# The first tile's output stored as two and six rows a partition instead of four and four

## The chip, the cores and the metric

The kernel runs on one core of one Trainium2 chip. The metric is the device time in microseconds (us) of one execution, as the median of several. A profile's span is about 1.3 us shorter than the time of the run (467.9 against 469.19 us in the profiled run of the kernel before), so spans are compared with spans and times with times.

## The reference

```python
# x: float32 (32, 512, 2048), i.e. 16384 rows of 2048
x1, x2 = x[..., :1024], x[..., 1024:]
gelu_x1 = 0.5 * x1 * (1 + erf(x1 / np.sqrt(2)))
return (gelu_x1 * x2).astype(np.float32)      # (32, 512, 1024)
```

134.22 MB are read and 67.11 MB written.

## The kernel before

Sixteen tiles, each of 128 partitions with 8 rows. Loads are issued by SP (`nc.sync`), stores by ACT (`nc.scalar`) up to tile 13, and by SP after that. ACT computes GELU, DVE (`nc.vector`) multiplies in place. There are two input and two output buffers, and the loads and stores of one buffer share the semaphore `ready[k]`.

```python
for ins in (
    load(0, slice(0, 4), first[0]),      # L0a: rows 0-3 of every partition
    load(0, slice(4, 8), first[1]),      # L0b
    load(1, slice(0, 8), ready[1]),      # L1
):
    ...
for i in range(n_tiles):
    k = i % 2
    last = i == n_tiles - 1
    pieces = i == 0 or last
    steps = ((0, 2), (2, 4), (4, 8)) if pieces else ((0, 5), (5, 8))
    for lo, hi in steps:
        ...                              # ACT: wait for the input, GELU of these rows
        ...                              # DVE: multiply these rows
        if pieces and hi % 4 == 0:
            if last:
                store(nc.sync, i, slice(hi - 4, hi), tail_stored)
            else:
                store(nc.scalar, i, slice(hi - 4, hi), ready[k])
    if not pieces:
        ...                              # store all 8 rows, tile 14 on nc.sync
    if i + 2 < n_tiles:
        nc.sync.wait_ge(mul_done, n[mul_done.name])
        load(i + 2, slice(0, R), ready[k])
```

`store` makes its queue wait for all multiplies issued so far. So the first store of tile 0 follows the multiply of rows 2-3, the second that of rows 4-7.

Of the kernel before, what the change touches and what calls it, by code (L numbers as in the profile page):

```python
# [1 line left out]

# [4 lines left out]

GELU = mybir.ActivationFunctionType.Gelu


@with_exitstack
def kernel(
    ctx: ExitStack,
    tc: tile.TileContext,
    x: bass.AP,
    out: bass.AP,
):
    nc = tc.nc
    P = nc.NUM_PARTITIONS

    x_flat = x.flatten_outer_dims()
    out_flat = out.flatten_outer_dims()
    n_rows, dim = x_flat.shape
    half = dim // 2

    R = 8
    x_t = x_flat.rearrange("(n p r) d -> n p r d", p=P, r=R)
    o_t = out_flat.rearrange("(n p r) d -> n p r d", p=P, r=R)
    n_tiles = x_t.shape[0]
    x_bufs = [nc.alloc_sbuf_tensor(f"x{k}_tile", [P, R, dim], x.dtype) for k in range(2)]  # L30
    o_bufs = [nc.alloc_sbuf_tensor(f"o{k}_tile", [P, R, half], out.dtype) for k in range(2)]



    first = [nc.alloc_semaphore(f"first{j}") for j in range(2)]
    ready = [nc.alloc_semaphore(f"ready{k}") for k in range(2)]
    gelu_done = nc.alloc_semaphore("gelu_done")
    mul_done = nc.alloc_semaphore("mul_done")
    tail_stored = nc.alloc_semaphore("tail_stored")
    n = {sem.name: 0 for sem in [*first, *ready, gelu_done, mul_done, tail_stored]}  # L40

    def counted(ins, sem, by):
        ins.then_inc(sem, by)
        n[sem.name] += by

    def load(i, rows, sem):
        ins = nc.sync.dma_start(out=x_bufs[i % 2][:, rows, :], in_=x_t[i][:, rows, :])  # L47
        counted(ins, sem, 16)
        return ins

    def store(queue, i, rows, sem):
        queue.wait_ge(mul_done, n[mul_done.name])
        counted(
            queue.dma_start(out=o_t[i][:, rows, :], in_=o_bufs[i % 2][:, rows, :]), sem, 16
        )




    for ins in (  # L60
        load(0, slice(0, 4), first[0]),
        load(0, slice(4, 8), first[1]),
        load(1, slice(0, 8), ready[1]),
    ):
        tc.no_tile_sem_insts.add(ins.ins.name)
    tc.close()
    tc.compile()  # L67
# [7 lines that stand above are left out]
            rows = slice(lo, hi)  # L75
            if i == 0 and lo % 4 == 0:
                nc.scalar.wait_ge(first[lo // 4], 16)
            elif lo == 0:
                nc.scalar.wait_ge(ready[k], n[ready[k].name])
            counted(  # L80
                nc.scalar.activation(  # L81
                    out=o_bufs[k][:, rows, :], in_=x_bufs[k][:, rows, :half], func=GELU
                ),
                gelu_done,
                1,
            )
            nc.vector.wait_ge(gelu_done, n[gelu_done.name])
            counted(
                nc.vector.tensor_mul(  # L89
                    out=o_bufs[k][:, rows, :],  # L90
                    in0=o_bufs[k][:, rows, :],
                    in1=x_bufs[k][:, rows, half:],
                ),
                mul_done,
                1,
            )
            if pieces and hi % 4 == 0:
                if last:
                    store(nc.sync, i, slice(hi - 4, hi), tail_stored)
                else:  # L100
                    store(nc.scalar, i, slice(hi - 4, hi), ready[k])
        if not pieces:
            if i == n_tiles - 2:
                store(nc.sync, i, slice(0, R), tail_stored)
            else:
                store(nc.scalar, i, slice(0, R), ready[k])
# [5 lines that stand above are left out]
    nc.scalar.drain()  # L112
    for sem in (*first, *ready):
        nc.scalar.sem_clear(sem)
    nc.vector.drain()
    nc.vector.sem_clear(gelu_done)
    nc.sync.sem_clear(mul_done)
    nc.sync.wait_ge(tail_stored, n[tail_stored.name]).then_inc(
        tail_stored, -n[tail_stored.name]
    )  # L120


# [1 line left out]
_INS = ['x']  # L124
_OUTS = [((32, 512, 1024), 'float32')]


# [23 lines left out]
```

## Time and profile before

| | before |
|---|---|
| time, median of 3 runs | 469.26 us (469.24 to 469.31) |
| span of the profiled execution | 467.9 us |
| busy DVE, ACT | 30%, 25% of the span |
| packets of the two data queues | 99.7% of 16 DMA engines' span |
| period of a middle tile | 29.0 us |

Read the queues first: their packets fill 99.7% of the DMA engines' span, and no compute engine is busy for more than 30% of it. The prediction below shows the lines for that. These two lines of the timeline of the kernel before (start, length, engine, line, what) are the last stores and the last tile's GELUs:

```profile
432.86 27.74 SPq L54 DMA_DIRECT2D out_dram<-o_tile  x3
448.56 7.21 ACT L81 ACTIVATE o_tile<-x_tile 128x2048 f32<-128x2048 f32 x3 [21.87 <-DMA out_dram<-o_tile]
```

The last tile's computing begins at 448.56, while tile 14's store, issued at 432.86, is still being moved.

### The profile page before, as it was taken

How to read it: one execution, taken by the hardware profiler on the slowest of the kernel's cores; microseconds unless marked ns; L12 is line 12 of the kernel's file. 1: busy time of each engine (PE TensorE's matmuls, PEld its weight loads, DVE VectorE, ACT ScalarE, POOL GpSimd, SP SyncE). 2: the span in 40 equal slices, each digit the busy share in tenths (PEclk: the TensorE clock that was granted, in tenths of full speed). 3: DMA queues.
4: the chain of work that ended last, by engine and by line, in shares of the span. 5: the costliest groups of instructions: out<-in, count | busy, mean ns of one | idle time of the engine just before them, and what ended most of it. 6: DMA issues, size and time to landing. Idle time of an engine off the chain costs nothing.

```text
span 467.9 us, 152 instructions
## 1 busy us (share of the span) xinstructions
DVE 140.5 (30%) x34; ACT 115.5 (25%) x35; POOL 0.2 (0%) x4
## 2 busy tenths in 40 slices
DVE  0330514207052060511606116060150702507043
ACT  1320606042060410604106050050500506014060
POOL 0000000000000000000000000000000000000000
DMA  8999999999999999999999999999999999999998
GB/s 359 448 448 443 403 405 492 409 403 448 459 437 403 434 417 493 403 403 448 476 420 403 445 406 493 403 406 445 487 409 403 445 451 448 403 434 417 493 389 373
DMA packets 5041, 201.34 MB, mean 430 GB/s; under 512 B 560, under 2 KB 560, under 8 KB 560
## 3 DMA queue, kind: packets, MB, share of 16 engines
q1 hardware_dynamic: 2880, 142.61, 70.6%
q10 hardware_dynamic: 2160, 58.72, 29.1%
q14 instruction: 1, 0.01, 0.0%
HBM read 134.22 MB, written 67.11 MB: 430 GB/s over the span
## 4 chain that ended last, share of the span: by engine, by line
DMA 76%; DVE 14%; ACT 8%; ACTq 0%; SPq 0%; issue 0%
DMA out_dram<-o_tile 66%; DVE o_tile L89 14%; DMA x_tile<-in_x_dram 10%; ACT o_tile L81 8%; ACTq L112 0%; SPq L47 0%
## 5 line engine op out<-in xcount | busy, mean ns | idle before, releaser
L89 DVE TENSOR_TENSOR o_tile<-o_tile,x_tile 128x5120 f32<-128x5120 f32 (+3 forms) x34 | 140.5, 4171 | 319.7 <-ACT o_tile L81 319.7
L81 ACT ACTIVATE o_tile<-x_tile 128x5120 f32<-128x5120 f32 (+3 forms) x34 | 114.3, 3407 | 337.4 <-DMA out_dram<-o_tile 301.6
L81 ACT ACT_TABLE_LOAD x1 | 1.3, 1283 | 2.9 <-PEq L67 2.9
L135 POOL MEMSET const-bfloat16-1.0<- 128x1 bf16 x1 | 0.1, 101 | 0.0
L135 POOL MEMSET const-uint8-127<- 128x1 uint8 x1 | 0.1, 101 | 0.0
L135 POOL MEMSET const-float32-0.0<- 128x1 f32 x1 | 0.1, 98 | 0.2 <-issue 0.2
L135 POOL MEMSET const-float32-1.0<- 128x1 f32 x1 | 0.1, 98 | 0.0
## 6 DMA issues: line engine op xcount, KB each, us to landing
out_dram<-o_tile ACTq DMA_DIRECT2D x13, 4096.0 KB, 44.7
x_tile<-in_x_dram SPq DMA_DIRECT2D x2, 4096.0 KB, 16.6
out_dram<-o_tile ACTq DMA_DIRECT2D x2, 2048.0 KB, 34.5
out_dram<-o_tile SPq DMA_DIRECT2D x1, 4096.0 KB, 25.2
out_dram<-o_tile SPq DMA_DIRECT2D x2, 2048.0 KB, 7.8
x_tile<-in_x_dram SPq DMA_DIRECT2D x15, 44.2
```

The costliest lines, as they stand in the source:

```text
L81: nc.scalar.activation(out=o_bufs[k][:, rows, :], in_=x_bufs[k][:, rows, :half], func=GELU),
L89: nc.vector.tensor_mul(out=o_bufs[k][:, rows, :], in0=o_bufs[k][:, rows, :], in1=x_bufs[k][:, rows, half:],),
L135: nc = _bacc.Bacc("TRN2", target_bir_lowering=False, num_devices=1)
```

## The change

The intent: get the first bytes of output on their way earlier. The first store no longer waits for rows 2-3. It takes rows 0-1 as soon as they are multiplied, and the second store takes the other six rows. The loads stay.

```diff
-            if pieces and hi % 4 == 0:
-                if last:
-                    store(nc.sync, i, slice(hi - 4, hi), tail_stored)
-                else:
-                    store(nc.scalar, i, slice(hi - 4, hi), ready[k])
+            if last and hi % 4 == 0:
+                store(nc.sync, i, slice(hi - 4, hi), tail_stored)
+            elif i == 0 and hi != 4:
+                store(nc.scalar, i, slice(0, 2) if hi == 2 else slice(2, 8), ready[k])
```

## The prediction

> **What bounds the kernel now.** I read the page first: the span, the busy shares and the DMA lines. Its columns are plain; q1 is the queue that SP issues to (all loads and the last three stores), q10 the one that ACT issues to (all other stores).
>
> ```profile
> span 467.9 us, 152 instructions
> ...
> DVE 140.5 (30%) x34; ACT 115.5 (25%) x35; POOL 0.2 (0%) x4
> ...
> q1 hardware_dynamic: 2880, 142.61, 70.6%
> q10 hardware_dynamic: 2160, 58.72, 29.1%
> ...
> HBM read 134.22 MB, written 67.11 MB: 430 GB/s over the span
> ```
>
> No compute engine is busy over 30%, and the two queues' packets fill 70.6 + 29.1 = 99.7% of the 16 DMA engines' span. Next the busy time by window (window, its length, DVE, ACT, POOL busy, TensorE clock, DMA share, GB/s), to see whether that average hides a slow stretch:
>
> ```profile
> 1.74:467.40 465.66, 140.49 (x34) 115.54 (x35) 0.00 (x0) 1.00 1.00 432
> 22.00:47.00 25.00, 4.42 (x1) 3.62 (x1) 0.00 (x0) 1.00 1.02 435
> 47.00:71.00 24.00, 8.76 (x2) 7.12 (x2) 0.00 (x0) 1.00 1.00 434
> 100.56:216.56 116.00, 35.04 (x8) 28.49 (x9) 0.00 (x0) 1.00 1.00 434
> 216.56:332.56 116.00, 35.04 (x8) 28.49 (x9) 0.00 (x0) 1.00 1.00 434
> ```
>
> From its first packet, at 1.74 us in the packet records, to the last, ending at 467.42, the DMA moves 432 GB/s, and 434 in the long middle. All bytes at 434 GB/s are 201.33 MB / 434 = 463.9 us. The span has 4.0 us more: 1.74 before the first packet, 0.45 after the last, and about 1.8 spread over the first and last stretches. So about 1.8 us (0.4%) is all that an earlier or later store could touch at all.
>
> The chain of waits (start, length, what) seems to say something else, and has to be read with care:
>
> ```profile
> 60.50 40.04 DMA out_dram<-o_tile
> 100.53 0.02 issue
> 100.56 4.48 ACT o_tile L81
> 105.03 0.02 issue
> 105.06 8.77 DVE o_tile L89 x2
> 113.83 0.02 issue
> 113.85 44.68 DMA out_dram<-o_tile
> ```
>
> It shows store, GELU, multiply, store. But the 44.68 us of a store are mostly queueing: a 4.19 MB store at 434 GB/s is 9.7 us of work. The period is 29.0 us a tile (100.56 to 129.57 in the timeline), which is 12.58 MB / 434 GB/s = 29.0. The compute pieces of this chain run while loads move; the chain names who let ACT go, not what is scarce.
>
> The start, from the timeline (start, length, engine, line, what, idle time before it in brackets):
>
> ```profile
> 12.76 3.71 ACT L81 ACTIVATE o_tile<-x_tile 128x2048 f32<-128x2048 f32 x2 [8.62 <-DMA x_tile<-in_x_dram]
> 14.70 4.49 DVE L89 TENSOR_TENSOR o_tile<-o_tile,x_tile 128x2048 f32<-128x2048 f32 x2 [14.70 <-ACT o_tile L81]
> 19.23 0.38 ACTq L54 DMA_DIRECT2D out_dram<-o_tile  x1
> 22.46 3.62 ACT L81 ACTIVATE o_tile<-x_tile 128x4096 f32<-128x4096 f32 x1 [5.99 <-DMA x_tile<-in_x_dram]
> 30.57 0.36 ACTq L54 DMA_DIRECT2D out_dram<-o_tile  x1
> ```
>
> The half-tile load ends at 12.7, two pieces are computed, the first half is stored from 19.23; the second from 30.57.
>
> [...] from about 24 to 71 us each engine alternates one 65,536-byte load packet (2.42 us) with one 16,384-byte store packet (0.61 us), 346 and 87 GB/s, which is 4:1. [...]
>
> **The change part by part.** Write L0a, L0b for the halves of tile 0's load, Lk for later loads, Sk for stores. Each DMA is 128 packets, 8 per engine, one for each partition, so packet size follows the rows per partition.
>
> Bytes: unchanged. Packets: still two stores of 128 for tile 0; 16 KB + 16 KB become 8 KB + 24 KB. From 0.611 us for 16 KB and 1.213 us for 32 KB the fixed part of a packet is 2 x 0.611 - 1.213 = 0.009 us. As the count stays, tile 0's stores cost each engine 8 x (0.611 + 0.611) = 9.8 us before and, by estimate, 8 x (0.31 + 0.91) = 9.8 after.
>
> First store: it follows the first multiply, 14.70 + 2.29 = 16.98, so it is issued at about 17.0, 2.2 us earlier. The order on ACT changes with it: this store now sits between the GELUs of rows 0-1 and rows 2-3, and ACT waits there for DVE. Rows 2-3 start at 17.0 + 0.38 = 17.4, where they started at 14.58: 2.8 us later. They end near 19.3 and their multiply near 21.5. That costs nothing, as rows 4-7 wait for L0b until 22.46.
>
> L0b: before, the first store packets came at 24.4, 5.2 us after the issue, though each engine's L0b was already over at about 21.8 and one L1 packet had slipped in. [...] Issued at 17.0 it gets 0 to 2 packets of 0.31 us in ahead of L0b's end. L0b lands 0 to 0.6 us later, and so do the GELU of rows 4-7 (22.5 to 23.1), S0b and the issue of L2 (30.6 to 31.2).
>
> L2's issue: L2 stands on SP's queue behind L1, whose packets last until about 46.6. It has 16 us to spare; 0.6 us is hidden.
>
> Pairing: before, S0a went beside L1, S0b beside L2, S1 beside L3 and so on, in step. If k = 0 to 2 packets of S0a (perhaps 3) go beside L0b, every later store runs k packets ahead of its load: L1 would end 1 to 3 us earlier (beside smaller store packets), L2 and all middle loads up to k x 1.21 = 2.4 to 3.6 us later, as each has let k more 32 KB packets by. In the steady state a store waits about 15 us on its queue before its first packet; being k x 3.63 us early leaves at least 4.
>
> The end: S14 is issued on SP's queue[...]. Whatever the pairing, what moves before L15 ends is L0 to L15 and S0 to S13, the same bytes, so L15 ends where it did, near 448. Then S14 (9.7 us alone) and both halves of S15 run. The last tile's first half store is issued at 455.03, while S14's packets last until about 457.6: 2.6 us to spare. If tile 15 now waits for L15 and no longer for S13, it starts up to 0.4 us earlier, which is hidden too.
>
> Sum: bytes 0, packets 0, rows 2-3 hidden, L0b's delay hidden, end 0. The first store's 2.2 us give nothing: the DMA had load packets to move in that time. Expected: 0.0 us, with some tenths for how the engines happen to line up.
>
> **The rivals.** First, the intent holds: writing starts 2.2 us sooner and the end comes 2.2 us sooner, 467.1 us. For it: there is about 1.8 us of lower rate at start and end. Against it: that is less than 2.2, part of it is the first packets and the last engines' finish, and no window has the DMA waiting for a store. A part of a dip just after L0b (about 0.3 us) could go: 468.9.
>
> Second, ACT's wait in the middle becomes the bound: rows 2-3 run past L0b's landing and the second half is late. It has 22.46 - 19.3 = 3.2 us to spare on ACT and 16 at L2's issue. Exposed in full, 2.8 us would give 472.1; I see no path for it.
>
> Third, packets of 8 KB cost more than their share. If each took 0.1 us more than 0.31, 8 of them per engine would cost 0.8 us: 470.1. Nothing measured here points to it.
>
> Fourth, the shifted pairing makes a hole later or exposes the last tile's compute. The spare times above (4 us a tile, 2.6 us at the end) speak against it; a hole of 1 us would give 470.3.
>
> **Range and chances.** The runs before differ by 0.07 us. I predict 469.2 us, from 468.6 (the dip goes, with some luck at the end) to 469.8 (dearer packets or a worse finish of the engines). 2% is 9.4 us; no rival comes near it. Faster 0.01, within 2% 0.98, slower 0.01.
>
> **What would show it.** Right: first store issued near 17.0, rows 2-3 starting near 17.4, rows 4-7 at 22.5 to 23.1, 434 GB/s in the middle, a 29.0 us period, some ACT waits naming the load where they named the store, the last GELUs at 448.1 to 448.6, and a span of 467 to 469. Wrong: a window after 22 us well below 434 GB/s, or the last store's issue after S14's end.

## The result

| | before | after |
|---|---|---|
| time, median of 6 runs | 469.25 us (469.17 to 469.39) | 469.88 us (469.65 to 470.47) |
| span of the profiled execution | 467.9 us | 468.5 us |
| last data packet ends (packet records) | 467.42 us | 468.06 us |

The ratio is 1.0014, with a 95% interval of 1.0001 to 1.0027. A ratio here is the mean time of one kernel's fast runs over that of the other's of the same rounds, so not quite the ratio of the medians. By the medians the change makes the kernel 0.63 us slower; no run of one kernel lies in the range of the other's. The prediction had said 469.2 us, and 469.8 at the most. It was wrong, by a loss of less than 0.2% that it did not see.

The page of the changed kernel looks almost the same:

```profile
span 468.5 us, 152 instructions
...
DVE 140.6 (30%) x34; ACT 115.7 (25%) x35; POOL 0.2 (0%) x4
...
q1 hardware_dynamic: 2880, 142.61, 70.6%
q10 hardware_dynamic: 2160, 58.72, 29.0%
```

Same packets, same bytes, the DMA still full (70.6 + 29.0 = 99.6%, against 99.7% before). The busy share can't show the loss: a packet that takes longer than usual counts as busy.

The issues of DMA in the page of the changed kernel (what, queue, count, KB each, us from issue to landing) show the two pieces:

```profile
out_dram<-o_tile ACTq DMA_DIRECT2D x1, 3072.0 KB, 42.6
out_dram<-o_tile ACTq DMA_DIRECT2D x1, 1024.0 KB, 25.3
```

The start in the changed kernel's timeline:

```profile
12.85 1.91 ACT L81 ACTIVATE o_tile<-x_tile 128x2048 f32<-128x2048 f32 x1 [8.71 <-DMA x_tile<-in_x_dram]
14.79 2.29 DVE L89 TENSOR_TENSOR o_tile<-o_tile,x_tile 128x2048 f32<-128x2048 f32 x1 [14.79 <-ACT o_tile L81]
17.12 0.38 ACTq L54 DMA_DIRECT2D out_dram<-o_tile  x1
17.54 1.91 ACT L81 ACTIVATE o_tile<-x_tile 128x2048 f32<-128x2048 f32 x1 [2.78 <-DVE o_tile L89]
19.48 2.29 DVE L89 TENSOR_TENSOR o_tile<-o_tile,x_tile 128x2048 f32<-128x2048 f32 x1 [2.40 <-ACT o_tile L81]
23.76 3.62 ACT L81 ACTIVATE o_tile<-x_tile 128x4096 f32<-128x4096 f32 x1 [4.30 <-DMA x_tile<-in_x_dram]
```

The first store is issued at 17.12 instead of 19.23. ACT waits 2.78 us for DVE in front of rows 2-3, as foreseen. But rows 4-7 start at 23.76 instead of 22.46: L0b landed 1.3 us later, where 0 to 0.6 had been predicted.

The chain of waits of the changed kernel (start, length, what) answers to the one of before:

```profile
60.57 42.87 DMA out_dram<-o_tile
...
103.47 4.48 ACT o_tile L81
...
116.76 44.68 DMA out_dram<-o_tile
...
161.47 4.48 ACT o_tile L81
```

Tile 3's GELU starts at 103.47 instead of 100.56, 2.9 us later. That is the shift of the pairing (each load lets more store packets by), not a loss: the period after it is still 29.0 us (161.47 - 103.47 = 58.0 for two tiles). The chain still names the store as what released ACT. Loads and stores of a buffer share one semaphore here, and the packet records say otherwise: at tile 2 the last packet of S0b (the second store of tile 0) ended at 66.6 and that of L2 at 72.9, and ACT went on at 74.47. The name on a shared semaphore has to be checked against the packets.

The busy time by window (window, length, DVE, ACT, POOL busy, TensorE clock, DMA share, GB/s) over the long middle is equal. Before:

```profile
50.00:448.00 398.00, 122.65 (x28) 96.92 (x28) 0.00 (x0) 1.00 1.00 433
```

After:

```profile
50.00:448.00 398.00, 122.65 (x28) 97.01 (x28) 0.00 (x0) 1.00 1.00 433
```

So the time was lost in the first 50 us and carried to the end. The tail of the changed kernel in its timeline:

```profile
435.76 25.32 SPq L54 DMA_DIRECT2D out_dram<-o_tile  x3
449.04 7.22 ACT L81 ACTIVATE o_tile<-x_tile 128x2048 f32<-128x2048 f32 x3 [19.45 <-DMA out_dram<-o_tile]
```

The last GELUs start 0.48 us later than before (449.04 against 448.56).

**Where in the first 50 us.** The packet records have the queue, size, start and duration of each packet. Most packets of one size take the same time in every trace: 0.309 us for 8 KB, 0.611 for 16, 0.912 for 24, 1.213 for 32, 2.418 for 64. The records do not name the DMA engine, but joining each packet to the one that starts where it ends gives one engine's sequence. One engine before (L = load, S = store, KB, start and duration in us; the 4-byte packets that end each transfer, 16 for each, are left out):

```
L32 19.22 1.21 | L32 20.43 1.21 | L64 21.65 2.80 | S16 24.45 0.61 | L64 25.05 2.44 | S16 27.49 0.61 | L64 28.10 2.42 | ...
... S16 42.67 0.61 | L64 43.27 2.42 | S16 45.69 0.61 | L64 46.31 2.43 | S16 48.73 0.61 | L64 49.34 2.42
```

One engine after:

```
L32 17.98 1.21 | L32 19.19 1.88 | L32 21.07 1.26 | S8 22.33 0.31 | S8 22.64 0.31 | L64 22.95 2.42 | S8 25.36 0.31 | ...
... S8 38.96 0.31 | L64 39.27 2.42 | L64 41.69 2.83 | S24 44.51 0.91 | S24 45.42 0.91 | L64 46.33 2.42 | S24 48.75 0.91
```

In both, a load packet shortly ahead of the first store's first packet is stretched: 2.80 us for 2.42 before, 1.88 for 1.21 after. All 16 engines show it; before, it is the last load packet ahead of the store, after, the last or the one before the last. In the changed kernel there is a second such place, 2.83 for 2.42, where the second store begins. Store packets are not stretched: the longest of the changed kernel takes what most of its size take, and in the kernel before none is more than 0.02 us over that. (Two store packets that seem to follow each other, as S8 at 22.33 and 22.64, have the 4-byte packet that ends the load between them.)

I call "loss" the duration of the packets above the median of their size in the same trace, summed over all packets that start in a stretch and divided by 16 engines. In the first place (17 to 30 us) it is 0.33 us before and 0.62 after, in the second (30 to 50 us) 0.06 and 0.34. Together that is 0.39 and 0.96: 0.57 us more, of the 0.64 us by which the last packet ends later. From 50 us on it is under 0.05 us in both. The mean end of the last 16 packets is 0.58 us later, so the rest is how unevenly the engines finish. The loss leaves out time in which an engine has no packet at all; between 3 and 460 us there is next to none in these two traces, where the packets' times add up to 100.2% of that stretch on 16 engines (the records overlap a little).

### The profile page after: what moved, and what is told of

The parts are those of the page before. It is cut to its first block, busy times and chain, and to the rows that moved or that the text cites. A ratio compares the mean times of both kernels' runs of the same rounds, so it can differ in the third digit from the quotient of the medians.

```text
span 468.5 us, 152 instructions
## 1 busy us (share of the span) xinstructions
DVE 140.6 (30%) x34; ACT 115.7 (25%) x35; POOL 0.2 (0%) x4
## 3 DMA queue, kind: packets, MB, share of 16 engines
q1 hardware_dynamic: 2880, 142.61, 70.6%
q10 hardware_dynamic: 2160, 58.72, 29.0%
## 4 chain that ended last, share of the span: by engine, by line
DMA 76%; DVE 14%; ACT 8%; ACTq 0%; SPq 0%; issue 0%
DMA out_dram<-o_tile 66%; DVE o_tile L89 14%; DMA x_tile<-in_x_dram 10%; ACT o_tile L81 8%; ACTq L111 0%; SPq L47 0%
```

## The experiments

Where five rounds were asked for, 4 to 6 runs gave times; in the last three kernels three rounds gave 4. Times of kernels of one group are compared with the kernel before in the same rounds: its medians were 469.16, 469.19, 469.27 and 469.35 us in the four groups. The losses come from each kernel's one trace, so a difference of some 0.1 us between two of them means little.

**The theories.** A: the first loss grows because the store stream starts while tile 0's second half is still loading. B: the sizes of the store packets, small ones or a step from small to large, cost. C: the loss at the first store is the first use of ACT's DMA queue. D: it is ACT's wait in the middle. And chance, which needs repeats.

### The changed kernel again (after_again), the kernel before again (before_again)

No edit.

> The changed kernel, unaltered, to see whether its 0.6 us is the same each time. The trace so far puts the loss into two places: load packets stretched beside the start of the first store (18 to 24 us from the span's start, 0.64 us against 0.32 before) and load packets stretched around the change from the first store to the second (39 to 47 us, 0.35 us against about 0). If these are properties of the kernel, 469.7 to 470.0 us and both places again. If they are chance, one or both are missing from this trace and the time nears 469.3 us.

Measured: 469.97 us (469.69 to 470.26) against 469.16; losses 0.48 and 0.48 us. Both places are there again, so they belong to the kernel. How they divide is not fixed.

> The kernel before, unaltered, for a second trace of its own. If its one loss at the first store (0.3 us at 21 to 27 us) and the absence of one at the second are properties of the kernel, both are seen again; time 469.1 to 469.4 us.

Measured: 469.27 us, the same as the other runs of before in these rounds, with one run at 471.43. Losses 0.26 and 0.08 us. The one loss at the first store is seen again, and none at the second.

### Two and six rows, but issued as late as before (late26)

```diff
-            elif i == 0 and hi != 4:
-                store(nc.scalar, i, slice(0, 2) if hi == 2 else slice(2, 8), ready[k])
+            elif i == 0 and hi != 2:
+                store(nc.scalar, i, slice(0, 2) if hi == 4 else slice(2, 8), ready[k])
```

> Two and six rows as in the change, but the first store waits for the multiply of rows 2-3, so it is issued near 19.2 us as before the change. Theory A (what costs is that the store stream starts while tile 0's second half is still loading): 469.2 to 469.35 us, first loss back to 0.3 us and, as the second store again starts with a new load, no second loss. Theory B (the small 8 KB packets, or the step from 8 KB to 24 KB, cost): the second loss of 0.35 us stays, 469.6 us or more.

Measured: 469.34 us (469.28 to 469.85) against 469.16. The time is in theory A's range, and its interval (ratio 0.9993 to 1.0018) includes no change at all. But A left no second loss, and the trace, of a run of 469.53 us, has one: first loss 0.10 us, second 0.61. In its timeline the first store and the GELU of rows 4-7 stand nearly where they stood before:

```profile
19.48 0.38 ACTq L54 DMA_DIRECT2D out_dram<-o_tile  x1
22.72 3.62 ACT L81 ACTIVATE o_tile<-x_tile 128x4096 f32<-128x4096 f32 x1 [6.00 <-DMA x_tile<-in_x_dram]
```

Neither theory is enough alone. Without the early start the first loss is even smaller than before (0.10 us with 8 KB store packets, 0.33 with 16); the second loss stays (0.61 us), so it has to do with sizes.

### Four and four rows, but issued as early as in the change (early16)

Wrong result: the first store takes zeros from the other output buffer, which nothing uses until tile 1.

```diff
+    nc.vector.memset(o_bufs[1][:, 0:4, :], 0.0).then_inc(filled, 1)
...
+            elif i == 0 and hi == 2:
+                nc.scalar.wait_ge(filled, 1)
+                nc.scalar.wait_ge(mul_done, n[mul_done.name])
+                nc.scalar.dma_start(out=o_t[0][:, 0:4, :], in_=o_bufs[1][:, 0:4, :]).then_inc(early, 16)
+            elif i == 0 and hi == 8:
+                store(nc.scalar, i, slice(4, 8), ready[k])
```

Tile 1's first GELU is made to wait for this store (`early`).

> Wrong result on purpose: four and four rows as in the kernel before, but the first store takes its four rows (zeros) from the other output buffer, so it can be issued at about 17.1 us, as in the change. 16 KB packets throughout. Theory A (early start costs): both losses come, 469.7 to 470.1 us. Theory B (small packets or the change of packet size cost): 469.2 to 469.35 us. If only the first loss comes: about 469.55 us.

Measured: 470.15 us (470.09 to 470.17) against 469.16. First loss 0.92 us, second 0: of theory A's two losses only the first came, and it was larger than supposed. Two load packets in a row were stretched on most engines, and three engines had no packet for 0.4 to 0.5 us, which adds 0.09 us to the mean. Its timeline:

```profile
17.29 0.38 ACTq L107 DMA_DIRECT2D out_dram<-o_tile  x1
24.91 3.62 ACT L86 ACTIVATE o_tile<-x_tile 128x4096 f32<-128x4096 f32 x1 [5.29 <-DMA x_tile<-in_x_dram]
```

Starting early costs by itself: 0.92 us in the first place, where the two traces of before have 0.26 and 0.33. L0b lands 2.4 us later than before; on the slowest engines two 16 KB store packets let by (1.2 us) are half of that. With late26 this is a square of two by two: late 16 KB 0.26 to 0.33, early 16 KB 0.92, late 8 KB 0.10, early 8 KB 0.48 to 0.64 us in the first place. The second place is all but empty for 16 KB after 16 and full for 24 KB after 8, early or late. In times, of the same rounds: late 16 KB 469.16, early 16 KB 470.15, late 8 KB 469.34, early 8 KB 469.97 us. So what is clear in the times is the early start, 0.6 to 1.0 us; the unequal sizes by themselves, late, cost 0.18 us, which is not clear of the noise. Their larger second loss is in part made up by a smaller first one.

### A tiny load first on ACT's queue (warm_before)

```diff
+    nc.scalar.dma_start(out=scrap[:, :], in_=x_t[0][:16, 0, :128]).then_inc(warmed, 16)
```

> The kernel before with one tiny load (16 partitions of 512 bytes) put on ACT's DMA queue at the start. Theory C (the first loss is the first use of ACT's queue): the 0.3 us dip at 21 to 27 us goes, about 469.0 us. If the dip belongs to the start of stores beside loads, it stays: 469.2 to 469.35 us.

Measured: 469.31 us (469.24 to 469.52) against 469.16; first loss 0.39 us. The queue was in use at the start, and the loss is still there. Theory C falls, as far as the queue goes; that the first write of a kernel costs is not tested by a load. The restart of the stores at 97 us in late_8_16, below, speaks against that.

### ACT's wait taken away (act_free)

The first store goes behind the GELU of rows 2-3 on ACT and waits for the first multiply alone.

```diff
+            if i == 0 and hi == 4:
+                store(nc.scalar, 0, slice(0, 2), ready[0])
             nc.vector.wait_ge(gelu_done, n[gelu_done.name])
...
-            elif i == 0 and hi != 4:
-                store(nc.scalar, i, slice(0, 2) if hi == 2 else slice(2, 8), ready[k])
+            elif i == 0 and hi == 8:
+                store(nc.scalar, i, slice(2, 8), ready[k])
```

> The changed kernel with the first store put after the GELU of rows 2-3 in ACT's order, still waiting for the first multiply alone: ACT's 2.8 us wait for DVE goes, the store is still issued at about 17.0 us. If ACT's wait is hidden, as predicted: 469.8 to 470.0 us, both losses as in the changed kernel. If the wait is what costs: 469.2 to 469.3 us.

Measured: 469.89 us (469.49 to 470.75) against 469.27; losses 0.64 and 0.26 us. Its timeline:

```profile
12.70 3.71 ACT L81 ACTIVATE o_tile<-x_tile 128x2048 f32<-128x2048 f32 x2 [8.57 <-DMA x_tile<-in_x_dram]
...
16.97 0.38 ACTq L54 DMA_DIRECT2D out_dram<-o_tile  x1
23.64 3.62 ACT L81 ACTIVATE o_tile<-x_tile 128x4096 f32<-128x4096 f32 x1 [7.24 <-DMA x_tile<-in_x_dram]
```

Both GELUs now run together, and rows 4-7 still start at 23.64, because the load is late. ACT's wait is hidden, as predicted. Theory D falls.

### Other sizes, all late (late35, late17, one8, late62)

The edits of the first two, against late26:

```diff
-                store(nc.scalar, i, slice(0, 2) if hi == 4 else slice(2, 8), ready[k])
+                store(nc.scalar, i, slice(0, 3) if hi == 4 else slice(3, 8), ready[k])   # late35
+                store(nc.scalar, i, slice(0, 1) if hi == 4 else slice(1, 8), ready[k])   # late17
```

> Late first store as before the change, pieces of three and five rows (12 KB and 20 KB packets). If the second loss grows with the step from the first store's packets to the second's (0 us for 16 to 16 KB, 0.6 us for 8 to 24 KB), it is about 0.3 us here, and the first loss about 0.2 us; time near 469.25 us. If any unequal split sets it off in full: 0.6 us, 469.4 us or more. If 24 KB packets alone do: no second loss, 469.1 us.

Measured: 469.43 us (469.16 to 469.47) against 469.19; losses 0.27 and 0.41 us. The second loss does not need 24 KB packets.

> Late first store, pieces of one and seven rows (4 KB and 28 KB packets). If the second loss grows with the step: 0.8 to 1.0 us, first loss about 0, time 469.4 to 469.6 us. If an unequal split costs a fixed amount: 0.6 us. If 24 KB packets alone do: no second loss, about 469.0 us.

Measured: 469.66 us (469.25 to 470.01) against 469.19; first loss 0, second 0.33, and 0.13 more after 50 us. The second loss does not grow with the step without end: 0.33 to 0.46 for 24 KB more, 0.61 for 16 KB more (late26).

In one8, tile 0 has one store of eight rows.

```diff
+            elif i == 0 and hi == 8:
+                store(nc.scalar, i, slice(0, 8), ready[k])
```

> Tile 0 stored in one piece of eight rows (32 KB packets) after its last multiply. If the loss at the start of the stores grows with the packet (0.1 us for 8 KB, 0.3 us for 16 KB): about 0.6 to 0.9 us at about 33 us, and 469.5 us. If what was lost in the first store is a fixed cost of starting: 0.3 us and 469.2 us. If starting later and beside 64 KB load packets costs nothing: 469.0 us.

Measured: 471.42 us (469.78 to 471.55) against 469.19, far above all three readings; one loss of 1.10 us at 31 to 37 us. The slowdown is twice the mean loss, as the loss was unequal: 15 engines had one stretched packet each and lost 0.9 to 1.2 us, but one engine had two, of 3.32 and 4.29 us, and lost 2.78. The engines' last packets ended between 467.90 and 469.49 us, where in the kernel before it was 466.92 to 467.42. The slowest engine sets the end. One of the four runs was at 469.78, and one run of the unaltered kernel at 471.43 (before_again), so the 2.2 us are less sure than the loss.

In late62 (wrong result) the first store, at the late time, takes six rows of zeros from the other buffer, the second the last two rows.

```diff
+            elif i == 0 and hi == 4:
+                ...
+                nc.scalar.dma_start(out=o_t[0][:, 0:6, :], in_=o_bufs[1][:, 0:6, :]).then_inc(early, 16)
+            elif i == 0 and hi == 8:
+                store(nc.scalar, i, slice(6, 8), ready[k])
```

> Wrong result on purpose: the first store, issued late (about 19.2 us), takes six rows of zeros from the other output buffer (24 KB packets), the second the last two rows (8 KB packets). If the loss at the first store is the time of one of its packets less 0.2 us, as 4 to 32 KB suggest, it is 0.91 - 0.2 = 0.7 us. If the second loss needs larger packets than the first store's, it is 0 here; if any change of size sets it off, 0.3 to 0.6 us. Time 469.5 to 469.7 us without a second loss, 470 us or more with it.

Measured: 469.40 us (469.35 to 469.76) against 469.27; losses 0.59 and 0. Here 8 KB packets after 24 KB ones cost nothing.

### Tile 1's load in halves (load1_halves, late26_halves)

```diff
-        load(1, slice(0, 8), ready[1]),
+        load(1, slice(0, 4), ready[1]),
+        load(1, slice(4, 8), ready[1]),
```

The load packets beside the first store are then 32 KB, as L0b's are, but the store still starts after L0b.

> The kernel before, except that tile 1's load comes in two halves, so that its packets are 32 KB like those of tile 0's halves. The first store starts as late as before, after tile 0's loads. If the larger first loss of the changed kernel comes from 32 KB load packets standing beside the first store packets, it appears here too: first loss 0.6 to 0.9 us against 0.3, about 469.5 to 469.9 us. If it comes from the earliness in itself (the second load of tile 0, the time since the start), the loss stays near 0.3 us and the time near 469.2 us.

Measured: 469.58 us (469.56 to 469.80) against 469.19; first loss 0.64 us where the kernel before has 0.26 to 0.33.

> Late first store of two rows (8 KB packets) and second of six, with tile 1's load in two halves, so that the first store's packets stand beside 32 KB load packets as in the changed kernel, but after tile 0's loads. If 32 KB load packets are what enlarges the first loss: 0.4 to 0.6 us. If the earliness is: 0.1 us, as with 64 KB load packets. A second loss may come as well; time 469.4 to 470 us.

Measured: 470.60 us (470.52 to 470.69) against 469.35; first loss 0.27, second 0.46 us. For 8 KB packets, too, 32 KB load packets raise the first loss (0.10 to 0.27), but not to the 0.48 to 0.64 of the changed kernel. So the size of the load packets is a part of what the early start brings, and not shown to be all. The time is worse than the losses say; its engines' last packets end between 467.45 and 469.01 us. The engine that ends last had no packet at all from 35.64 to 36.53 us, just after its last packet of the first store: a hole of 0.9 us on one engine of 16, which the loss does not count.

### Larger but a power of two; equal but not one (late_8_16, late_12_12)

The last two rows go on SP's queue behind tile 2's load, so that the first two stores can be chosen freely. That delays tile 2's GELU (to 81.6 us in both), so these two kernels are read for the second loss and not for their time.

```diff
-                store(nc.scalar, i, slice(0, 2) if hi == 4 else slice(2, 8), ready[k])
+                store(nc.scalar, i, slice(0, 2) if hi == 4 else slice(2, 6), ready[k])   # late_8_16
+                store(nc.scalar, i, slice(0, 3) if hi == 4 else slice(3, 6), ready[k])   # late_12_12
...
+            if i == 0:
+                store(nc.sync, 0, slice(6, 8), ready[0])     # late_12_12 the same
```

> Late first store of two rows (8 KB packets), second of four rows (16 KB), the last two rows stored on SP's queue behind tile 2's load. If the second loss needs packets larger than the first store's: 0.2 to 0.4 us at about 44 to 47 us. If it comes from sizes that are no power of two: 0. First loss 0.1 us in both. Read from the trace; the time is about 469.2 to 469.6 us.

Measured: 470.68 us (469.95 to 470.93) against 469.35; first loss 0.09, then 0.18 at 30 to 38 us (before the second store's packets), and 0.26 at 38 to 50.

> Late first store of three rows (12 KB packets), second of three rows too, the last two rows stored on SP's queue behind tile 2's load. If the second loss needs packets larger than the first store's: 0. If it comes from sizes that are no power of two: 0.2 to 0.5 us at about 45 to 48 us. First loss 0.25 us in both.

Measured: 470.49 us (469.76 to 471.58) against 469.35; first loss 0.17, then 0.28 at 30 to 38 us, and 0 at 38 to 50, where the second store begins.

Over all the traces read for it, the second loss came where the second store's packets were larger than the first's (0.26 to 0.61 us), and not where they were equal or smaller (0 to 0.08 us in the two traces of before, early16, late62 and late_12_12). The 12 KB packets of late_12_12, no power of two, did not set it off. The traces of late_8_16 and late_12_12 have more loss elsewhere, and the place at 97 us says something. Tile 2's late GELU left the stores with nothing to do from 81 to 100 us. Where they start again, with 32 KB packets, the last load packet ahead of them is stretched on all or nearly all engines, by 0.52 us in late_8_16 and 0.13 in late_12_12. So the loss came at a start of stores beside loads that was not the first of the kernel; its size differs much between two traces. The rest I can't place.

## Why the prediction was wrong

**What held.** The DMA bounds the kernel, and it has no idle time that an earlier store could fill: packets fill 99.7 and 99.6% of the engines' span, and the middle runs at 433 GB/s in both kernels. The first store came at 17.12 (predicted 17.0), ACT's stop and its cost of nothing held (act_free), and one or two packets got in ahead of L0b's end on each engine. Ahead of L1's first packet nine engines had let two store packets by and seven three: 2.4 on average, and 2.4 x 1.21 = 2.9 us is what the middle loads came later (predicted up to 2.4 to 3.6), without a change of the 29.0 us period. S14 came behind L15 on every engine: its first packet started 1.22 us after the engine's last packet of L15 before the change (one 32 KB store packet, 1.21 us, lies between) and 0.002 us after it in the changed kernel. S15's computing stayed behind S14's transfer.

**What held by luck or did not hold.** The number of packets ahead of L0b's end came out right on a wrong reading. My estimate was that a store's first packet comes at most about 2.6 us after its issue, worked out from the issue at 19.23 us and L0b's end at about 21.8. But before, all engines still took a load packet at 21.6 to 22.1 us, 2.4 to 2.8 us after the issue, and after, the earliest store packet came 4.0 us after it. With 4.0 us and no stretching no store packet would have come ahead of L0b's last 32 KB packet, which started at 20.4 to 20.9 us before (an estimate from these times); on seven engines one did. The wait of a store on its queue in the middle was 17.1 us (113.85 to 130.93), not about 15, and 10.0 us were left of it after (116.76 to 126.73), where at least 4 had been reckoned. L1 did not end 1 to 3 us earlier: tile 1's GELU began at 47.27 (47.20 before), as 24 KB packets of the second store already stood ahead of L1's end (the first started at 41.86 us, L1's last ended at 45.97, and at 46.22 before). The last GELUs came at 449.04, outside 448.1 to 448.6, and of the signs of being wrong, a window below 434 GB/s came: 429 GB/s from 20 to 50 us, and 446 before.

**The step that failed** is the sum: "bytes 0, packets 0, rows 2-3 hidden, L0b's delay hidden, end 0". Its term "packets 0" came from "tile 0's stores cost each engine 8 x (0.611 + 0.611) = 9.8 us before and, by estimate, 8 x (0.31 + 0.91) = 9.8 after". The store packets do take just that, 0.309 and 0.912 us. But I took it that their neighbours' durations do not change, and they do: load packets ahead of a starting store are stretched (2.80 us for 2.42, 1.88 for 1.21, 2.83 for 2.42 on the engines shown). The two places measured 0.96 us in the changed kernel instead of 0.39. "End 0" failed only by this: what moves before S14 ended at 448.66 us instead of 448.02, the loss carried on. The same omission made "L0b lands 0 to 0.6 us later" too small; the stretching came on top of the packets, and it was 1.3.

The trace of before had shown the clue. The prediction knew of "a dip just after L0b (about 0.3 us)" and counted it only as something that could go away. It is the loss at the first store, beside loads (0.33 us in that trace, 0.26 in before_again), and the change started that stream in a worse place and gave it a second start. The third rival, dearer small packets, was wrong in its reason (8 KB packets took 0.309 us each, as reckoned) and only by coincidence not far in its time (470.1).

**The intent** found nothing to gain, for the predicted reason: the engines had load packets to move (at 21.6 to 22.1 us, after the first store's issue at 19.23, all 16 still took one).

**What stays open** is why load packets are stretched. Beside 64 KB load packets the late first losses are 0 us for 4 KB packets, about 0.1 for 8, 0.2 to 0.3 for 12, 0.3 to 0.4 for 16, 0.6 for 24 and 1.1 for 32. That is one store packet's own time (0.16, 0.31, 0.46, 0.61, 0.91 and 1.21 us) less 0.1 to 0.35. Why that is, no record here shows; the restart at 97 us (0.52 and 0.13 us for 32 KB packets) does not fit this series, and it is not shown either why tile 1's 32 KB packets cost nothing after any first tile, even after the 8 KB of late62 (433 GB/s from 50 to 448 us, as in the kernel before). No version that beats the kernel before came out of it: the first two places together lost 0.33 us at the least among correct kernels with another split (late17), against 0.35 to 0.39 before, and late17 lost 0.13 more later.

## What to carry to other kernels

When the DMA engines are full, as here, sending a piece earlier changes the order of packets and not their number (2880 and 2160 on the two queues in both kernels); ask then what the new neighbours do to each other. At a start of a second stream look at the durations of the packets that were there first, not only at busy shares, which count a stretched packet as work (99.7 and 99.6% here, with 0.39 and 0.96 us lost). Here equal pieces, started after the first small loads were over, did best, though late unequal pieces were not clearly worse in time (0.1 to 0.5 us), and one large first piece was the worst (2.2 us in the median).
